# Down rows dealt by the load, block products that add on in PSUM, and one split for two token tiles

## The chip, the cores and the metric

The kernel runs on one core of one Trainium2 chip. A core has a tensor engine (PE, with the weight loads shown apart as PEld), a vector engine (VectorE, DVE in the profile), a scalar engine (ScalarE, ACT), GpSimd (POOL) and SyncE (SP), which here issues nearly all transfers. Transfers run on 16 DMA engines. The time is device microseconds for one execution of the program, and the kernel before takes 1070.54 us (median of three runs, 1070.43 to 1071.01).

## The reference

Two layers work on 256 tokens of 1024 features. Each layer has a feed-forward block, a mixer (gated short convolution, a chunked linear recurrence, multi-scale pooling), cross attention to 256 memory rows, and a second feed-forward block; each of the four ends in a residual and a layer normalization. All inputs and weights are 32-bit floats.

```python
def swiglu(x, w_gate, w_up, w_down):
    return (jax.nn.silu(x @ w_gate) * (x @ w_up)) @ w_down
...
    h = x
    for l in range(DEPTH):
        h = layer_norm(ALPHA * h + 0.5 * swiglu(h, ffn1_gate[l], ffn1_up[l], ffn1_down[l]),
                       ln_g[l, 0], ln_b[l, 0])
        z = h @ w_in[l]
...
        mix = jnp.concatenate([y_conv, y_rec, y_pool], axis=-1) @ w_out[l]
        h = layer_norm(ALPHA * h + mix, ln_g[l, 1], ln_b[l, 1])
        h = layer_norm(ALPHA * h + cross_attn(h, mem, ca_q[l], ca_k[l], ca_v[l], ca_o[l]),
                       ln_g[l, 2], ln_b[l, 2])
        h = layer_norm(ALPHA * h + 0.5 * swiglu(h, ffn2_gate[l], ffn2_up[l], ffn2_down[l]),
                       ln_g[l, 3], ln_b[l, 3])
    return h
```

The inner width of a feed-forward block (FFN) is 2816: gate and up are 1024 x 2816, down is 2816 x 1024. The change touches the four FFNs, and in one place the loading of the memory rows.

## The kernel before

**Split numbers.** Every operand of a large product is kept as a high part in a reduced format (`hi`, written by ScalarE as a cast) and a low part (`lo`, the rest, subtracted by VectorE). `split` (L60 to L62) issues the two. A product of two such operands is three matmuls: high by high, high by low, low by high (`mm_rows`). `product` walks the moving operand so that neighbouring columns of PSUM come from the two halves of the weight columns: column c of the first half and column c of the second half lie beside each other.

**Loads.** `load` fetches a weight block in tiles of 128 partitions x 1024 numbers (512 KB), two to a call's step. They land in a ring of six `raw` buffers; each is split into `whi` and `wlo`, rings of eight. A load is issued by SP in the order of the program, waits there until its `raw` buffer is free, and holds back the loads and the small transfers that stand behind it on SP. For the down weights one tile is 128 neighbouring rows of 4 KB.

**An FFN in chunks.** The width is cut into five chunks of 512 columns and one of 256. For most chunks (`first`, `hidden`) PE makes the gate product (48 matmuls for both token tiles of 128) and the up product (48). `activate` (L436) writes Silu of the gate sums from PSUM to `sg`, and `gated` (L440) multiplies by the up sums. Both do so in two instructions for a token tile, because the order of the columns in PSUM and the order wanted in `sg` don't fit one access pattern. Then `turn` transposes: four small SP transfers (128 KB each) deal `sg` out over the partitions into the tile `dealt`, VectorE transposes 32 x 32 blocks into `square`, and `split` makes the high and low parts `ah`, `al` for the down product. It does this for one token tile after the other.

**Down products.** `both(c, u)` multiplies half a chunk (two tiles of down rows, 24 matmuls) into four sums `dn` that stay in PSUM through the FFN. The half chunks are interleaved with the products of later chunks. The last three (both halves of chunk 4, the first of chunk 5, the 256 wide one) are kept for `tail`, which `finish` calls for each token tile and each half of the columns; one such call reads all six remaining down tiles, then the normalization of that part follows.

**Chunks by seven products.** Chunk 4 (and chunk 2 in three of the four FFNs) is made by `by_seven`: two token tiles against gate and up, seen as a product of 2 x 2 blocks, by seven block products in place of eight. `bx` holds sums and differences of blocks of x; `parts_of` adds weight blocks in place (L597) and splits them. A product (`run`) is 12 matmuls into a PSUM tile. `put` (L619) adds or subtracts a product from PSUM to a 512 wide tile in SBUF. Four products go into four PSUM tiles; three more go into new ones of the same ring of four, and are added to the sums in SBUF by `left`, after which Silu and the multiplication follow in another tile `sg`, and `turn`.

**What sets the order.** A scheduler puts the instructions of each engine into one order before the run; the engines keep that order and wait for each other by semaphores. The order for the matmuls of the mixer and of the kernel's start is written by hand.

## Time and profile before

| | before |
|---|---|
| median of three runs | 1070.54 us |
| profiled execution, span | 1068.8 us |
| PE busy | 1059.3 us (99%), 5966 matmuls |
| DVE busy | 946.3 us (89%) |
| ACT busy | 642.4 us (60%) |
| DMA, mean rate | 217 GB/s |
| DMA queue of SP and its kind, share of 16 engines | 64.8% |

The span runs from the first to the last instruction of the profiled execution; the device time of the runs lies some 2 us above it. Busy time counts an engine's instructions, and for PE neighbouring matmuls overlap. In a row of the groups of instructions the line comes first, then the engine, the operation, what it writes and reads (`whi<-raw`), the shapes and the count; behind the first bar busy time and the mean of one in ns, behind the second the idle time of the engine just before these instructions and what ended it. The chain of waits lists the work that ended last, followed back from the end. In a row of stretches the two last numbers are the share of the 16 DMA engines that was busy and the GB/s moved.

### The profile page before, as it was taken

The page shows a single profiled execution, that of the slowest core. Times are in us where ns is not written, and L with a number is a line of the kernel's source. Part 1 is how long each engine was busy: PE and PEld are TensorE (multiplying, and loading weights), DVE is VectorE, ACT ScalarE, POOL GpSimd, SP SyncE. Part 2 cuts the span into 40 slices and gives each one's busy share as a digit, 9 for nine tenths or more (in the row PEclk, how much of TensorE's full clock was granted, in tenths as well). Part 3 has the DMA queues.
Part 4 walks back from the last instruction along what each step waited for, and adds up shares of the span by engine and source line. Part 5 has one row for each costly group of instructions (what it writes and reads, how often), then busy time and mean ns, then how long its engine had stood idle before and what let it go on. Part 6 is the DMA issues. An engine that isn't in the chain of part 4 may idle for free.

```text
span 1068.8 us, 16312 instructions
## 1 busy us (share of the span) xinstructions
PE 1059.3 (99%) x5966; PEld 937.7 (88%) x5966; DVE 946.3 (89%) x1318; ACT 642.4 (60%) x916; POOL 66.4 (6%) x114
## 2 busy tenths in 40 slices
PE   9999999999999999999999999999999999999997
PEld 7888888889899888888888888888898998888886
DVE  6977997998988799999799999788989787999996
ACT  7555664666557565656575557566764665656660
POOL 9700001000000000000000000010000000000000
PEclk9999999999999999999999999999999999999999
DMA  9997484755574575848675865856536665759461
GB/s 362 262 307 256 129 288 165 249 176 174 170 278 167 178 252 194 290 167 218 238 272 184 256 254 183 290 179 216 196 126 213 241 227 181 257 156 334 134 223 40
DMA packets 130895, 231.90 MB, mean 217 GB/s; under 512 B 9408, under 2 KB 48608, under 8 KB 130816
## 3 DMA queue, kind: packets, MB, share of 16 engines
q1 hardware_dynamic: 129024, 228.49, 64.8%
q0 software_dynamic: 1216, 1.20, 0.5%
q8 instruction: 47, 0.77, 0.3%
q10 hardware_dynamic: 576, 1.18, 0.3%
q14 instruction: 32, 0.26, 0.1%
HBM read 216.15 MB, written 1.05 MB: 203 GB/s over the span
## 4 chain that ended last, share of the span: by engine, by line
PE 99%; DMA 0%; DVE 0%; issue 0%; DVEq 0%
PE acc L105 65%; PE dn L105 31%; PE acc L172 1%; PE dn L923 1%; PE dn L982 0%; DMA h<-in_x_dram 0%; PE acc L491 0%; PE dn L981 0%; PE dn L971 0%; PE acc L1047 0%; PE dn L888 0%; DVE h L358 0%; DVE h L353 0%; PE dn L472 0%; DVE st L338 0%
## 5 line engine op out<-in xcount | busy, mean ns | idle before, releaser
L61 ACT CAST whi<-raw 128x1024 fp32r<-128x1024 f32 (+1 forms) x438 | 442.9, 1042 | 197.5 <-DVE raw L597 54.9
L62 DVE TENSOR_TENSOR wlo<-raw,whi 128x1024 fp32r<-128x1024 f32 (+1 forms) x438 | 515.7, 1209 | 32.6 <-ACT whi L61 29.0
L105 PE MATMUL acc<-whi,xT 128*128 128x512 f32 x1032 | 312.9, 380 | 0.0
L105 PEld LDWEIGHTS acc<-whi,xT 128*128 128x128 f32 x1032 | 195.1, 189 | 27.5
L105 PE MATMUL acc<-wlo,xT 128*128 128x512 f32 x516 | 195.6, 379 | 0.0
L105 PE MATMUL acc<-xT,whi 128*128 128x512 f32 x576 | 142.3, 383 | 0.2
L105 PE MATMUL dn<-whi,ah 128*128 128x512 f32 x346 | 131.5, 380 | 0.0
L105 PE MATMUL dn<-wlo,ah 128*128 128x512 f32 x346 | 131.2, 379 | 0.0
L105 PE MATMUL dn<-whi,al 128*128 128x512 f32 x346 | 131.2, 379 | 0.0
L105 PEld LDWEIGHTS acc<-xT,whi 128*128 128x128 f32 x576 | 104.0, 190 | 12.5 <-ACT whi L61 0.7
L105 PEld LDWEIGHTS acc<-wlo,xT 128*128 128x128 f32 x516 | 97.5, 189 | 13.8
L105 PE MATMUL dn<-whi,xT 128*128 128x512 f32 x288 | 87.9, 381 | 0.0
L105 PEld LDWEIGHTS acc<-xT,wlo 128*128 128x128 f32 x576 | 75.5, 191 | 3.9
L105 PE MATMUL acc<-xT,wlo 128*128 128x256 f32 x576 | 75.9, 275 | 0.0
L105 PEld LDWEIGHTS dn<-whi,al 128*128 128x128 f32 x346 | 65.4, 189 | 9.2
L105 PEld LDWEIGHTS dn<-wlo,ah 128*128 128x128 f32 x346 | 65.4, 189 | 9.2
L105 PEld LDWEIGHTS dn<-whi,ah 128*128 128x128 f32 x346 | 65.4, 189 | 9.1
L350 POOL TENSOR_TENSOR rs<-rs,nhalf 128x1 f32<-128x1 f32 x16 | 14.9, 930 | 833.6 <-DVE rs L346 598.1
L597 DVE TENSOR_TENSOR raw<-raw 128x1024 f32<-128x1024 f32 x56 | 66.2, 1217 | 0.4
L105 PEld LDWEIGHTS dn<-whi,xT 128*128 128x128 f32 x288 | 54.4, 189 | 7.7 <-DVE xT L62 0.3
L105 PE MATMUL dn<-wlo,xT 128*128 128x512 f32 x144 | 54.6, 379 | 0.0
L332 DVE SCALAR_TENSOR_TENSOR h<-h,dn 128x512 f32<-128x512 f32 x31 | 21.2, 683 | 32.9 <-PE dn L105 32.9
(234 smaller groups left out, 1277.5 us busy)
## 6 DMA issues: line engine op xcount, KB each, us to landing
raw<-in_ffn_up_dram SPq DMA_DIRECT2D x88, 512.0 KB, 5.3
raw<-in_ffn_down_dram SPq DMA_DIRECT2D x88, 512.0 KB, 6.6
raw<-in_ffn_gate_dram SPq DMA_DIRECT2D x84, 512.0 KB, 5.1
raw<-in_w_in_dram SPq DMA_DIRECT2D x48, 512.0 KB, 4.7
dealt<-sg SPq DMA_DIRECT2D x80, 128.0 KB, 4.7
raw<-in_ca_k_dram SPq DMA_DIRECT2D x16, 512.0 KB, 4.9
raw<-in_w_out_dram SPq DMA_DIRECT2D x16, 512.0 KB, 4.5
raw<-in_ca_v_dram SPq DMA_DIRECT2D x16, 512.0 KB, 5.3
```

What stands on the lines that cost most here:

```text
L61: nc.scalar.copy(hi, src)
L62: lows.append(nc.vector.tensor_tensor(lo, src, hi.bitcast(F32), op=ALU.subtract))
L105: nc.tensor.matmul(o, w, x, start=start, stop=stop)
L172: nc.tensor.transpose(pt[:, k, :], src[:, (4 * j + k) * P : (4 * j + k + 1) * P], unit)
L332: nc.vector.scalar_tensor_tensor(v, v, ALPHA / scale, sums(y[i][n]), op0=ALU.mult, op1=ALU.add, accum_out=None if junk is None else st[:, ...
L350: nc.gpsimd.tensor_tensor(rs, rs, nhalf[:, 0:1], op=ALU.pow)
L597: nc.vector.tensor_tensor(r[i], r[i], plus[i], op=ALU.add)
L923: nc.tensor.matmul(o[g, hh, :], kc[:, hh, g], x, start=True, stop=True)
```

## The change

Four things change together.

1. *Down rows.* For chunks 0 to 4 a down tile no longer holds 128 neighbouring rows. `load` gets a flag `dealt`: of 256 rows, tile b takes the rows a*64 + b*32 + j, with a from 0 to 3 and j from 0 to 31. With the inner index in this order, `activate` and `gated` write `sg` in one pattern, one instruction for a token tile.
2. *Block products.* Products five to seven start from what stands in PSUM (`more`, no start flag) and add onto products one, three and four there. The order of the three becomes: gate's lower block, up's lower block, the sum of blocks. Two additions to SBUF tiles go away, e and f lie in one tile `ef`, and the last multiplication is done for both tiles in one instruction, in place in `sg`.
3. *Turn.* The transposes of both token tiles write one tile, and one `split` follows.
4. *Tiles.* The pool's two `up` buffers of 512 numbers become one of 1024, which `square`, `halves`, `up` and the memory rows' `turned` share.

```diff
-    def load(src, k0, nk, c0, ncol, fine=False):
+    def load(src, k0, nk, c0, ncol, fine=False, dealt=False):
...
             for b in range(0, step, part):
-                loads.append(nc.sync.dma_start(
-                    raw[b // half][:, b % half : b % half + part, :],
-                    src[(a + b) * P : (a + b + part) * P, c0 : c0 + ncol].rearrange("(k p) c -> p k c", p=P),
-                ))
+                to = raw[b // half][:, b % half : b % half + part, :]
+                if dealt:
+                    rows = src[a * P : (a + step) * P, c0 : c0 + ncol].rearrange("(a k j) c -> k a j c", a=4, j=32)
+                    loads.append(nc.sync.dma_start(to[:, 0, :], rows[b]))
+                else:
+                    loads.append(nc.sync.dma_start(
+                        to, src[(a + b) * P : (a + b + part) * P, c0 : c0 + ncol].rearrange("(k p) c -> p k c", p=P)
+                    ))
...
             def ordered(v):
-                return v.rearrange("p (a k j) -> p k a j", a=4, j=32)
-
-            def by_two(v, o):
-                o = o.rearrange("p (n a j m) -> p m n a j", n=2, a=4, m=2)
-                return [(ordered(v)[:, 2 * m : 2 * m + 2], o[:, m]) for m in range(2)]
+                return v.rearrange("p (a m q) -> p a m q", a=4, m=2)
+
+            def in_order(o):
+                return o.rearrange("p (a q m) -> p a m q", a=4, m=2)
 
             def activate(s, i, og):
-                for v, o in by_two(s[:, i, :], og):
-                    nc.scalar.activation(v, o, AF.Silu)
+                nc.scalar.activation(ordered(s[:, i, :]), in_order(og), AF.Silu)
 
             def gated(s, i, ou):
-                for v, o in by_two(s[:, i, :], ou):
-                    nc.vector.tensor_tensor(v, o, v, op=ALU.mult)
+                v = ordered(s[:, i, :])
+                nc.vector.tensor_tensor(v, in_order(ou), v, op=ALU.mult)
...
+                d = fp.tile([P, NT, 4, P], F32, tag="up", name="square", bufs=1)
                 for i in range(NT):
-                    d = fp.tile([P, 4, P], F32, tag="up", name="square")
                     nc.vector.transpose(
-                        d.rearrange("p k (b r) -> p b k r", b=4), x[:, :, i, :].rearrange("p b (k j) -> p b k j", k=4)
+                        d[:, i].rearrange("p k (b r) -> p b k r", b=4),
+                        x[:, :, i, :].rearrange("p b (k j) -> p b k j", k=4),
                     )
-                    split(ah[:, :, tok(i)], al[:, :, tok(i)], d)
+                d = d.rearrange("p i k t -> p k i t")
+                split(*(y.rearrange("p k (i t) -> p k i t", i=NT) for y in (ah, al)), d)
...
                 s = activations()
+                ef = fp.tile([P, NT, CHUNK], F32, tag="up", name="halves", bufs=1)
+                e, f = ef[:, 0, :], ef[:, 1, :]
                 o = [acc((P, CHUNK)) for _ in range(4)]
                 run(o[0], part_of_x(0, 0), parts_of(w00))
                 run(o[2], bx[0], parts_of(w00, w01))
+                nc.scalar.copy(ordered(s[:, 0, :]), in_order(o[0]))
                 run(o[1], bx[1], parts_of(w00, w11))
-                e = half_sum()
-                put(e, o[1], ALU.add, g[0])
+                put(s[:, 0, :], o[1], ALU.add, s[:, 0, :])
                 run(o[3], bx[2], parts_of(w01, w11))
-                put(g[1], o[3], ALU.add, e)
-                f = half_sum()
-                put(f, o[2], ALU.subtract, g[1])
-                put(e, o[2], ALU.subtract, e)
-                o = [acc((P, CHUNK)) for _ in range(3)]
-                run(o[0], bx[3], parts_of(w11))
-                run(o[1], part_of_x(0, 1), parts_of(w10))
-                run(o[2], part_of_x(1, 1), parts_of(w00, w10))
+                put(s[:, 1, :], o[3], ALU.add, s[:, 0, :])
+                put(f, o[2], ALU.subtract, s[:, 1, :])
+                run(o[0], part_of_x(0, 1), parts_of(w10), True)
+                run(o[2], bx[3], parts_of(w11), True)
+                run(o[3], part_of_x(1, 1), parts_of(w00, w10), True)
 
                 def left():
-                    put(e, o[0], ALU.add, e)
-                    for i in range(NT):
-                        put(g[i], o[1 + i], ALU.add, g[i])
-                    s = fp.tile([P, NT, CHUNK], F32, tag="spare2", name="sg", bufs=1)
-                    for i, u in enumerate((e, f)):
-                        v = ordered(s[:, i, :])
-                        nc.scalar.activation(v, g[i].rearrange("p (k a j) -> p k a j", a=4, j=32), AF.Silu)
-                        nc.vector.tensor_tensor(v, v, u.rearrange("p (k a j) -> p k a j", a=4, j=32), op=ALU.mult)
+                    put(e, o[2], ALU.subtract, s[:, 0, :])
+                    put(s[:, 1, :], o[3], ALU.add, s[:, 0, :])
+                    activate(s, 0, o[0])
+                    nc.scalar.activation(s[:, 1, :], s[:, 1, :], AF.Silu)
+                    nc.vector.tensor_tensor(s, s, ef, op=ALU.mult)
                     return turn(s)
...
             def slab(c, u):
-                w = load(down, c * 4 + 2 * u, 2, 0, DM)
+                w = load(down, c * 4 + 2 * u, 2, 0, DM, dealt=c < len(chunks) - 1)
```

More of the change, by code (lines that the diff above doesn't have):

```diff
@@ L100, in halves, with product @@
         )
-    def product(o, w, x, start, stop):
+    def product(o, w, x, start, stop, more=False):
         x = x.rearrange("p (h c) -> p c h" if len(x.shape) == 2 else "p r (h c) -> p r c h", h=2)
         o = o.rearrange("p (c h) -> p c h" if len(o.shape) == 2 else "p r (c h) -> p r c h", h=2)
-        nc.tensor.matmul(o, w, x, start=start, stop=stop)
+        nc.tensor.matmul(o, w, x, start=start, stop=stop, skip_group_check=more)
     def sums(o):
@@ L126, in add, with mm_rows @@
         nc.vector.tensor_tensor(dst, o[:, 0], dst, op=ALU.add)
-    def mm_rows(o, xh, xl, wh, wl, start, stop):
-        product(o, xh, wh, start, False)
-        product(o, xh, wl, False, False)
-        product(o, xl, wh, False, stop)
+    def mm_rows(o, xh, xl, wh, wl, start, stop, more=False):
+        product(o, xh, wh, start, False, more)
+        product(o, xh, wl, False, False, more)
+        product(o, xl, wh, False, stop, more)
     def tok(i):
@@ L608, in part_of_x, with run @@
                     return xTh[:, d, tok(i)], xTl[:, d, tok(i)]
-                def run(o, x, w):
+                def run(o, x, w, more=False):
                     for k in range(4):
                         wh, wl = w.at(k, slice(0, CHUNK))
-                        mm_rows(o, x[0][:, k, :], x[1][:, k, :], wh, wl, k == 0, k == 3)
-                def half_sum():
-                    return fp.tile([P, 4, P], F32, tag="up", name="half").rearrange("p k t -> p (k t)")
+                        mm_rows(o, x[0][:, k, :], x[1][:, k, :], wh, wl, k == 0 and not more, k == 3, more)
@@ L618, in put @@
                 def put(o, a, op, b):
-                    nc.vector.tensor_tensor(halves(o), sums(a), halves(b), op=op)
+                    nc.vector.tensor_tensor(ordered(o), in_order(a), ordered(b), op=op)
                 s = activations()
-                g = [s[:, i, :] for i in range(NT)]
+                ef = fp.tile([P, NT, CHUNK], F32, tag="up", name="halves", bufs=1)
+                e, f = ef[:, 0, :], ef[:, 1, :]
                 o = [acc((P, CHUNK)) for _ in range(4)]
                 run(o[0], part_of_x(0, 0), parts_of(w00))
-                nc.scalar.copy(halves(g[0]), sums(o[0]))
```

8 lines of the change are left out of this document (4 added, 4 removed).

## The prediction

> **What bounds the kernel now.** I read the page from its head to the chain, then the waits of the tensor engine, then the transfers.
>
> ```profile
> span 1068.8 us, 16312 instructions
> PE 1059.3 (99%) x5966; PEld 937.7 (88%) x5966; DVE 946.3 (89%) x1318; ACT 642.4 (60%) x916; POOL 66.4 (6%) x114
> ...
> PEclk9999999999999999999999999999999999999999
> ...
> DMA packets 130895, 231.90 MB, mean 217 GB/s; under 512 B 9408, under 2 KB 48608, under 8 KB 130816
> ...
> q1 hardware_dynamic: 129024, 228.49, 64.8%
> ...
> PE 99%; DMA 0%; DVE 0%; issue 0%; DVEq 0%
> ```
> ```profile
> 1057.48 4.03 PE acc L105 x36
> ```
> ```profile
> PE dn L472 <- DVE kTh L467: 1.5, 1, 1.5
> PE acc L491 <- DMA h<-in_x_dram: 0.5, 1, 0.5
> ```
>
> The chain is PE for 99% of the span, at a full granted clock, the second fence is its last stretch of PE work (start, length), and the third the whole list of PE's waits: two, at the start. All that is not PE busy is 1068.8 - 1059.3 = 9.5 us, 7.3 of them after that last stretch, at 1061.5, in the final normalization and the output. The profiled execution (1068.8 us of span) lies 1.7 us below the median of 1070.54, so the sum is made as an addition and put on the median. The matmuls are the same in number and shape after the change. So it can win little; it loses where a weight tile comes late. That turns the question to the loads, which take 64.8% of 16 DMA engines as a mean.
>
> **What the edits take off the vector and scalar engines** (groups, kept apart by shape):
>
> ```profile
> L62 DVE TENSOR_TENSOR wlo<-raw,whi 128x1024 fp32r<-128x1024 f32 x430 | 510.4, 1219 | 32.5 <-ACT whi L61 29.0 <-PE acc L105 1.9
> L597 DVE TENSOR_TENSOR raw<-raw 128x1024 f32<-128x1024 f32 x56 | 66.2, 1217 | 0.4
> L62 DVE TENSOR_TENSOR al<-square,ah 128x512 fp32r<-128x512 f32 x40 | 25.7, 682 | 0.4
> L440 DVE TENSOR_TENSOR sg<-acc,sg 128x256 f32<-128x256 f32 x52 | 19.3, 415 | 0.0
> L619 DVE TENSOR_TENSOR half<-acc,sg 128x512 f32<-128x512 f32 x14 | 9.6, 684 | 0.0
> L649 DVE TENSOR_TENSOR sg<-sg,half 128x512 f32<-128x512 f32 x14 | 9.3, 685 | 0.4 <-ACT sg L648 0.4
> ...
> L61 ACT CAST whi<-raw 128x1024 fp32r<-128x1024 f32 x430 | 438.2, 1049 | 197.2 <-DVE raw L597 54.9 <-PE dn L105 53.5 <-PE acc L105 35.5
> L61 ACT CAST ah<-square 128x512 fp32r<-128x512 f32 x40 | 24.3, 621 | 19.0 <-DVE square L453 18.9
> L436 ACT ACTIVATE sg<-acc 128x256 f32<-128x256 f32 x48 | 16.0, 382 | 5.7 <-PE acc L105 5.5
> ```
>
> - One eviction for a token tile: 52 of 0.415 us become 26 of about 0.684 (the 512-wide product from PSUM), -3.8 us on DVE; 52 Silu halves of 0.382 (these 48 and 4 more of another pool) become 26 of at most 0.621, -3.7 us on ACT.
> - Products that add on in PSUM: each of 7 block-product chunks loses 2 of its 7 512-wide additions, 14 x 0.684 = -9.6 us; its two multiplications of 0.685 become one of about 1.217, -1.1 us.
> - One split for both token tiles: 40 x 0.682 to 20 x 1.219, -2.9 us on DVE; 40 x 0.621 to 20 x 1.049, -3.9 us on ACT. Both transposes now precede the split, which delays the first half by under 2 us; its reader comes a projection later (over 10 us).
>
> Together some -17.4 us on DVE and -7.6 on ACT, costed at nothing, since PE is the cover and does not wait for them. If that cover goes, it goes because PE and DVE wait for loads, and then less DVE work does not shorten the wait.
>
> **The accumulation's new waits.** Product six now adds onto the sum that the fourth addition (f) still reads, so after product four two additions must be through before it, with one weight split between them in the changed order: 2 x 0.684 + 1.219 = 2.6 us, and product five covers 12 matmuls of 0.216 = 2.6 us. Before, two products covered three additions. I take 0; the other end is another split in front, 1.2 us x 7 = 8.5 us.
>
> **The moved rows of the down weights.** This is the part that decides. 80 of the 88 down loads keep bytes, row length and their issuer, SP, but read four runs of 32 rows, 64 rows apart: the source's outermost count goes from 128 to 4. No load of the trace has such a pattern; the outermost counts on SP's queue are 128 or, at the dealt tiles, 32. The list of issues (the first two rows and the last of 28, 586 issues in all; the last figure is the median to landing):
>
> ```profile
> raw<-in_ffn_up_dram SPq DMA_DIRECT2D x88, 512.0 KB, 5.3
> raw<-in_ffn_down_dram SPq DMA_DIRECT2D x88, 512.0 KB, 6.6
> ...
> rows<-in_pool_scale_dram POOLq DMA_DIRECT2D x1, 2.0 KB, 4.8
> ```
>
> The page's 9408 packets under 512 B are 16.05 for each issue, which I read as one completion write per engine and transfer: so far every transfer uses all 16. So the price lies between 16 engines (nothing changes) and one engine for each outermost row block, four. Rates per engine come from three stretches:
>
> ```profile
> 1033.50:1039.50 6.00, 6.00 (x38) 5.49 (x37) 5.50 (x8) 4.71 (x7) 0.00 (x0) 1.00 0.66 271
> 970.00:990.00 20.00, 20.00 (x94) 17.54 (x93) 17.43 (x17) 13.13 (x17) 0.00 (x0) 1.00 1.02 368
> 990.00:1010.00 20.00, 20.00 (x95) 17.51 (x94) 19.97 (x24) 11.51 (x13) 0.00 (x0) 1.00 0.25 77
> ```
>
> The last two columns are the share of the 16 engines and GB/s. Down rows of 4 KB: 271/16/0.66 = 25.7 GB/s for an engine; the mix with 2 KB rows: 22.5; mostly dealt tiles: 19.3. A 512 KB load gives 32,768 B to each of 16 engines, 1.28 us (down) or 1.45 (gate, up); on four it gives 131,072 B, 5.1 us, while the others idle. I take four: what all the listed hardware-queue loads share, counts on both sides that 16 divides, is what this one loses.
>
> The Trainium skill has a rule for it (DMA: Bandwidth & Descriptors, the section Why a DMA increments its semaphore by 16 and not by 1): a transfer runs on the largest number of engines up to 16 that divides the outermost counts of both sides. By it 128 and 4 give four engines; the 16 small packets per issue agree with it for the old patterns, and no run here yet shows four.
>
> Now one FFN, with each engine serving its queue in order. Where the first changed load is issued, and where PE needs the last:
>
> ```profile
> 24.99 1.59 SPq L77 DMA_DIRECT2D raw<-in_ffn_down_dram  x2
> ...
> 387.39 2.08 SPq L77 DMA_DIRECT2D raw<-in_ffn_down_dram  x2
> ...
> 554.97 2.08 SPq L77 DMA_DIRECT2D raw<-in_ffn_down_dram  x2
> ...
> 913.69 2.08 SPq L77 DMA_DIRECT2D raw<-in_ffn_down_dram  x2
> ...
> 994.05 2.61 SPq L450 DMA_DIRECT2D dealt<-sg  x4
> ```
> ```profile
> 155.68 18.13 PE dn L105 x84
> ...
> 514.34 18.13 PE dn L105 x84
> ...
> 681.97 18.13 PE dn L105 x84
> ...
> 1040.64 16.84 PE dn L105 x78
> ```
> ```profile
> raw<-in_ca_o_dram SPq DMA_DIRECT2D x16, 512.0 KB, 3.8
> ```
>
> The second fence starts with a half chunk of down products (24 matmuls, 18.13/84 = 0.216 us each, 5.2 us), and then the tail, whose first sum reads all of its six tiles within 18 matmuls: the last at +15 x 0.216 = 3.2 us. So PE needs the last tile at 164.1, 522.8, 690.4 and 1049.1: 139.1, 135.4, 135.4 and 135.4 us after the first changed issue. In that time the four engines must pass 20 changed loads, 20 x 5.1 = 102.2 us; 28 of gate and up, 28 x 1.45 = 40.6; two down and two normalization loads, 5.1; and 20 dealt tiles of 8,192 B per engine, 0.43 each, 8.5: 156.4 us. Add the fixed part of a load (3.8 - 1.28 = 2.5 us), cast and split (1.05 + 1.22): 161.2 us. The last tile is late by 22.1 us once and 25.8 three times, **99.5 us**. The lead of loads over PE is already spent in this: it stands in the window. With 16 engines the same work is 80 us, in a window of 135.
>
> Then the dealt tiles stand in the same queues. The one issued at 994.05 has 13 changed loads, some 21 others and 12 dealt ahead of it since 914.7: 66 + 30 + 5 us, so it lands near 1020, where its transposes ran here:
>
> ```profile
> 1003.02 1.30 DVE L453 STREAM_TRANSPOSE square<-dealt 128x512 f32<-128x512 f32 x2
> ```
> ```profile
> 1008.93 0.33 SPq L77 DMA_DIRECT2D raw<-in_ffn_down_dram  x1
> ```
>
> DVE stands there some 17 us, with the block product's splits queued behind it in order, and with them the release of the raw buffer for the next down load, 5.9 us after the transposes in this trace (1008.93, below). Of those 17 us only what empties the queues counts: they run dry at 1020 plus two normalization loads, 1022.6, and are fed again at 1026 plus 1.0: 4.4 us, four times, **17.6 us**. The price of a cold PE after its waits I bound by the start's row, 7 x (0.651 - 0.380) = 1.9 us, four times **7.6 us**, and zero:
>
> ```profile
> L472 PE MATMUL dn<-kTh 128*128 128x512 f32 x7 | 3.7, 651 | 1.5 <-DVE kTh L467 1.5
> L105 PE MATMUL dn<-whi,ah 128*128 128x512 f32 x346 | 131.5, 380 | 0.0
> ```
>
> Issuing: the new pattern may take SP what a dealt tile takes, 2.61/4 = 0.65 us; 20 in an FFN are 13 us in 135, behind transfers of 5.1 us each, so nothing.
>
> Sum: 99.5 + 17.6 + 7.6 = 125 us, and 1070.5 + 125 = 1195; the 28 gate and up loads at 25.7 GB/s too (0.17 us less each, 19 us in four FFNs) would make it 1176, and I take a value nearer to the sum, **1190 us**.
>
> **Rivals.**
> 1. The split over the engines does not follow the outermost count, and all 16 are used: then nothing on the path changes, 1070 us. For it: bytes and row lengths are the same. Against: nothing in the trace but the missing example. It decides if 8 engines or more are used, since 20 x 2.55 + 54.2 = 105 us fits the window.
> 2. Faster, by DVE's 17.4 us: PE would have to be waiting for DVE. Its list of waits has 2.0 us at the start, and of the 9.5 us without PE most are the first loads and the last normalization; 9.5 - 7.3 = 2.2 us at most, 1068.4, and part of that is the start.
> 3. 16 engines, but the accumulation's wait comes out at its upper end: 1079 us. For it: DVE is 89% busy and in order.
> 4. Four engines that keep only the mean rate of the whole run: 228.49 MB/(16 x 0.648 x 1068.8 us) = 20.6 GB/s. The window's 3.83 MB per engine take 186 us, 30 more per FFN, 1310 us. Against: that mean is of 16 engines crowding one memory.
>
> **How the numbers follow.** Four engines as summed 0.80, rival 1 0.10, rival 2 0.02, rival 3 0.03, rival 4 0.05. The likeliest alone spans 1100 (three quarters of the lateness made up by loads that start earlier than those of this trace, no cold clock) to 1285 (most of the way to rival 4); 1078 to 1285 takes in rival 3 and leaves some 2 in 10 out. Faster by over 0.2% (2.1 us, about what a measurement here can tell) is rival 2's 0.02, the same is rival 1's 0.10, slower is the rest, 0.88.
>
> **What would show it.** Packets under 512 B fall by 80 x 12 = 960 to about 8450; the changed loads' median to landing rises from 6.6 us to well over 10; PE waits for ACT and DVE on down tiles at the four tails, 20 to 30 us each, and its granted clock dips there; DVE waits for dealt tiles. DVE's busy time falls by some 17 us. The prediction is wrong if the small packets stay at 9408, or if the queues turn out to be fed so far ahead that the tails find their tiles.

## The result, and the profile after

The changed kernel takes **1305.13 us** (median of 4 runs, 1302.22 to 1315.31), the kernel before in the same session 1070.76 us (1070.43 to 1071.01). The ratio is 1.220, with a 95% interval of 1.217 to 1.223: 234 us slower. The forecast was 1190 us, 120 us slower, with 1078 to 1285 around it: the direction was right, the size was half of what was measured, and the time lies outside the range.

The page of the changed kernel, the lines that answer to those of before (busy times and their share; the granted clock in 40 slices; packets; the load queue; the chain by engine and by line):

```profile
span 1302.8 us, 16237 instructions
...
PE 1138.3 (87%) x5966; PEld 972.3 (75%) x5966; DVE 937.0 (72%) x1251; ACT 632.8 (49%) x870; POOL 66.2 (5%) x114
...
PEclk9898987999999999979699997969999999999798
...
DMA packets 129935, 231.90 MB, mean 178 GB/s; under 512 B 8448, under 2 KB 47648, under 8 KB 129856
...
q1 hardware_dynamic: 128064, 228.49, 55.9%
...
PE 41%; DMA 30%; DVE 15%; SPq 7%; issue 3%; ACT 3%; DVEq 0%; ACTq 0%
PE acc L110 27%; DMA raw<-in_ffn_down_dram 18%; PE dn L110 12%; DVE wlo L62 7%; SPq L453 7%; DMA dealt<-sg 6%; DMA raw<-in_ffn_gate_dram 5%; DVE raw L602 2%; ACT whi L61 2%; DMA raw<-in_ffn_up_dram 1%; DVE al L62 1%; DVE square L456 1%; DVE sg L443 1%; PE acc L177 1%; DVE sg L621 0%
```

The chain was PE for 99% of the span; now PE holds 41% of it and transfers 30%, the down loads alone 18%. The small packets are 8448, which is 9408 less 80 x 12: each of the 80 changed loads writes 4 completions and not 16. The bytes are the same. PE's busy time rose by 79.0 us for the same 5966 matmuls, while its granted clock dips (line PEclk; its mean is 0.928, against 0.998 before). The waits of the changed kernel (waiter, its line, releaser: total us, times, longest):

```profile
ACT whi L61 <- DMA raw<-in_ffn_down_dram: 221.5, 48, 11.1
DVE wlo L62 <- ACT whi L61: 199.6, 78, 5.7
...
DVE square L456 <- DMA dealt<-sg: 62.5, 14, 11.3
```
```profile
PE dn L110 <- ACT ah L61: 67.2, 12, 12.2
PE acc L110 <- DVE wlo L62: 27.7, 9, 8.1
PE acc L110 <- DVE sg L621: 23.6, 7, 4.3
PE dn L110 <- ACT whi L61: 11.1, 7, 2.2
```

The two waits for transfers in the kernel before:

```profile
ACT whi L61 <- DMA raw<-in_ffn_down_dram: 20.3, 15, 3.7
...
DVE square L453 <- DMA dealt<-sg: 7.8, 4, 3.6
```

ACT waits 222 us for down tiles (20 before), VectorE waits for ACT, VectorE stands 63 us for dealt tiles (8 before), and PE, which waited for nothing after the start, now waits for ACT and VectorE. The third PE row is of another kind: PE waits until VectorE has read a sum onto which a product is to be added. The end of the chain (start, length, what):

```profile
1246.71 3.93 SPq L453
1250.64 0.05 issue
1250.69 2.77 SPq L453
...
1254.16 6.24 SPq L453
...
1260.50 14.21 DMA raw<-in_ffn_down_dram
```

The last changed load is issued at 1260.50 and takes 14.2 us. Ahead of it SP stood in the issues of four dealt tiles. They are the last four of their FFN; in the kernel before, the last four (1025.67, line 450 there) took 2.64 us in all:

```profile
1245.88 14.52 SPq L453 DMA_DIRECT2D dealt<-sg  x4
```
```profile
1025.67 2.64 SPq L450 DMA_DIRECT2D dealt<-sg  x4
```

Of SP's 544 issues, 66 lasted longer than 1.5 us, 222.6 us in all; before, 3 did, 4.7 us.

So the candidates for the 234 us were: the four engines' work; SP's standing in line; the way the dealt tiles wait; the accumulation; and PE's slower clock. The experiments take the first and the fourth apart from the rest. No run changes the clock alone.

### The profile page after: what moved, and what is told of

Its sections match the earlier page's. It is cut to its first block, busy times and chain, and to the rows that moved or that the text cites. A ratio compares the mean times of both kernels' runs of the same rounds, so it can differ in the third digit from the quotient of the medians.

```text
span 1302.8 us, 16237 instructions
## 1 busy us (share of the span) xinstructions
PE 1138.3 (87%) x5966; PEld 972.3 (75%) x5966; DVE 937.0 (72%) x1251; ACT 632.8 (49%) x870; POOL 66.2 (5%) x114
## 2 busy tenths in 40 slices
DMA packets 129935, 231.90 MB, mean 178 GB/s; under 512 B 8448, under 2 KB 47648, under 8 KB 129856
## 3 DMA queue, kind: packets, MB, share of 16 engines
q0 software_dynamic: 1216, 1.20, 0.5%
## 4 chain that ended last, share of the span: by engine, by line
PE 41%; DMA 30%; DVE 15%; SPq 7%; issue 3%; ACT 3%; DVEq 0%; ACTq 0%
PE acc L110 27%; DMA raw<-in_ffn_down_dram 18%; PE dn L110 12%; DVE wlo L62 7%; SPq L453 7%; DMA dealt<-sg 6%; DMA raw<-in_ffn_gate_dram 5%; DVE raw L602 2%; ACT whi L61 2%; DMA raw<-in_ffn_up_dram 1%; DVE al L62 1%; DVE square L456 1%; DVE sg L443 1%; PE acc L177 1%; DVE sg L621 0%
## 5 line engine op out<-in xcount | busy, mean ns | idle before, releaser
L110 PE MATMUL acc<-whi,xT 128*128 128x512 f32 x1032 | 320.6, 385 | 30.1 <-DVE sg L621 23.6
L110 PEld LDWEIGHTS acc<-whi,xT 128*128 128x128 f32 x1032 | 197.6, 191 | 62.5 <-issue 31.9
L110 PE MATMUL dn<-whi,ah 128*128 128x512 f32 x346 | 147.8, 427 | 78.3 <-ACT ah L61 67.2
L110 PE MATMUL dn<-whi,al 128*128 128x512 f32 x346 | 146.3, 423 | 6.1 <-DVE al L62 6.1
L110 PE MATMUL dn<-wlo,ah 128*128 128x512 f32 x346 | 146.5, 423 | 4.7 <-DVE wlo L62 4.7
L110 PEld LDWEIGHTS dn<-whi,ah 128*128 128x128 f32 x346 | 73.9, 214 | 98.3 <-ACT ah L61 73.0
L110 PEld LDWEIGHTS dn<-whi,al 128*128 128x128 f32 x346 | 73.1, 211 | 24.2 <-DVE al L62 12.9
L110 PEld LDWEIGHTS dn<-wlo,ah 128*128 128x128 f32 x346 | 73.6, 213 | 19.8 <-DVE wlo L62 8.2
L110 PE MATMUL acc<-wlo,kTh 128*128 128x512 f32 x112 | 50.6, 452 | 27.2 <-DVE wlo L62 27.1
L456 DVE STREAM_TRANSPOSE square<-dealt 128x512 f32<-128x512 f32 x40 | 26.0, 689 | 62.5 <-DMA dealt<-sg 62.5
L355 POOL TENSOR_TENSOR rs<-rs,nhalf 128x1 f32<-128x1 f32 x16 | 14.9, 930 | 1058.2 <-DVE rs L351 770.7
```

The costliest lines, as they stand in the source:

```text
L110: nc.tensor.matmul(o, w, x, start=start, stop=stop, skip_group_check=more)
L355: nc.gpsimd.tensor_tensor(rs, rs, nhalf[:, 0:1], op=ALU.pow)
L456: nc.vector.transpose(d[:, i].rearrange("p k (b r) -> p b k r", b=4), x[:, :, i, :].rearrange("p b (k j) -> p b k j", k=4),)
```

## The experiments

### The other parts of the change: plain rows

```diff
-                w = load(down, c * 4 + 2 * u, 2, 0, DM, dealt=c < len(chunks) - 1)
+                w = load(down, c * 4 + 2 * u, 2, 0, DM, dealt=False)
```

The order of instructions on every engine is that of the changed kernel.

> The changed kernel with the down rows fetched in plain order (the pairing of rows and activations is left out, so the output differs); all other parts of the change stand. Theory: the other parts cost and bring next to nothing, 1068 to 1071 us. Rival (the accumulation's wait or the shared buffers cost): 1079 us or more. Rival (they bring DVE's 17 us): 1054 to 1066 us.

Measured 1082.2 us, ratio 1.0108 (1.0093 to 1.0123): the second reading. The rest of the change costs 11.6 us. PE's waits, the whole list of this run, and its busy line:

```profile
PE acc L110 <- DVE halves L621: 5.3, 7, 0.8
PE acc L110 <- DVE sg L621: 2.6, 7, 0.4
PE dn L477 <- DVE kTh L472: 1.5, 1, 1.5
PE acc L496 <- DMA h<-in_x_dram: 0.5, 1, 0.5
```
```profile
PE 1063.0 (98%) x5966; PEld 937.2 (87%) x5966; DVE 935.5 (87%) x1251; ACT 639.2 (59%) x870; POOL 66.4 (6%) x114
```

The last two rows were there before. The first two are new, 7 times each, once for each block-product chunk: the two accumulating products whose sums VectorE still reads. They stop PE for 7.9 us, and PE is busy 3.7 us longer (1063.0 against 1059.3): 11.6 us, the whole difference of the two spans (1080.4 less 1068.8).

### The accumulation alone

The edit to the kernel with plain rows (lines that only write to another tile are left out):

```diff
...
-                run(o[0], part_of_x(0, 1), parts_of(w10), True)
-                run(o[2], bx[3], parts_of(w11), True)
-                run(o[3], part_of_x(1, 1), parts_of(w00, w10), True)
...
+                o = [acc((P, CHUNK)) for _ in range(3)]
+                run(o[0], part_of_x(0, 1), parts_of(w10))
+                run(o[1], bx[3], parts_of(w11))
+                run(o[2], part_of_x(1, 1), parts_of(w00, w10))
...
+                    put(e, o[1], ALU.add, e)
+                    for i in range(NT):
+                        put(s[:, i, :], o[2 * i], ALU.add, s[:, i, :])
...
```

> The changed kernel with plain rows (pairing left out), and the three late products in PSUM sums of their own again, added on VectorE as before the change; one pattern, one split and the shared buffers stay. Theory (the 11.6 us that plain rows leave are PE's wait until VectorE has read a sum onto which a product is to be added): 1069 to 1071 us. Rival (they come from the shared buffers or the one split for both token tiles): 1080 to 1083 us.

Measured 1071.25 us, ratio 1.0003 (0.9994 to 1.0011). The loss of plain rows went with the accumulation. The scheduler's order changes with the edit too, but the list of waits above names the same cause, and here PE's waits are again the two of the start. The one eviction pattern, the one split and the shared buffers together cost and bring nothing that can be measured.

### The loads alone, in the kernel before

The load function of the changed kernel in the kernel before; nothing else:

```diff
-                w = load(down, c * 4 + 2 * u, 2, 0, DM)
+                w = load(down, c * 4 + 2 * u, 2, 0, DM, dealt=c < len(chunks) - 1)
```

> The kernel before, with one edit: the down loads of all chunks but the last fetch four runs of 32 rows (rows and activations paired wrongly). Theory: the loads alone carry the whole loss, 1300 to 1310 us. Rival (half of the loss is from the other parts, the forecast of 1190 was right for the loads): about 1190 us.

Measured 1292.7 us, ratio 1.207 (1.206 to 1.209), 222 us over before, with every engine's instructions in the order of the kernel before. This is 7 us under the range that was expected, which gave the loads the whole loss. With plain rows the rest of the change costs 11.6 us, and the four-run loads add 222.9 to that (1305.1 less 1082.2). The two parts add up.

### How many engines: 2, 8 and 16

```diff
-                    rows = src[...].rearrange("(a k j) c -> k a j c", a=4, j=32)
+                    rows = src[...].rearrange("(a k j) c -> k a j c", a=8, j=16)
```

with a=16, j=8 and a=2, j=64 in the two other runs. The orders of instructions on all engines are those of the changed kernel.

> The changed kernel, where a changed load fetches eight runs of 16 rows instead of four runs of 32 (so rows and activations are paired wrongly; sizes, bytes, instructions and their order are those of the changed kernel). Theory (the outermost count of the source sets how many engines serve a load, and their work is what delays): 8 engines, 65,536 B each, 2.55 us at 25.7 GB/s; 20 x 2.55 + 54.2 = 105 us of engine work per FFN in a window of 135: about 1070 us, at most 1075. Rival (a source in runs is slow in itself, or slow to issue, whatever the number of engines): no better than the changed kernel, about 1300 us. Rival (the extra over the forecast is SP's waiting at each load that is not yet taken): some tens of us above 1070, 1090 to 1150.

> The changed kernel, where a changed load fetches sixteen runs of 8 rows (rows and activations paired wrongly; all else as in the changed kernel). Theory (number of engines): 16 engines as before, 1066 to 1070 us, and the packets under 512 B are 9408 again. Rival (runs are slow in themselves): near 1300 us.

> The changed kernel where a changed load fetches two runs of 64 rows (rows paired wrongly): two engines, 262,144 B each, 10.2 us a load at 25.7 GB/s. Theory (engine time): in the changed kernel's fourth FFN the load queue was busy 168 us of 173; each of 20 loads is 5.1 us longer, 102 us an FFN, 408 us in all: 1700 to 1730 us. Rival (the loss grows with the loads' own share of packets, slower at fewer engines): above 1800.

The packets of the three runs, of 8, 16 and 2 runs in a load:

```profile
DMA packets 130256, 231.90 MB, mean 203 GB/s; under 512 B 8769, under 2 KB 47969, under 8 KB 130177
```
```profile
DMA packets 130896, 231.90 MB, mean 213 GB/s; under 512 B 9409, under 2 KB 48609, under 8 KB 130817
```
```profile
DMA packets 129775, 231.90 MB, mean 140 GB/s; under 512 B 8288, under 2 KB 47488, under 8 KB 129696
```

The small packets are 9408 less 80 x 8, 0 and 14, to within one: a source with an outermost count of 8, 16 or 2 runs on 8, 16 or 2 engines. This is the rule of the Trainium skill (DMA: Bandwidth & Descriptors, Why a DMA increments its semaphore by 16 and not by 1), and four runs here agree with it. The times are 1143.7, 1091.4 and 1661.1 us. All three miss what the theory gave (at most 1075; at most 1070; 1700 to 1730). Eight engines should have fitted the window and lost 61.5 us over plain rows. That time lies in the range of the third reading, SP's waiting, but SP's issues over 1.5 us are 12 there, 34.6 us in all, and the run down_on_pool below speaks against it too. That the number of engines orders the loss is shown; the sum that turns it into time was wrong. What the trace's packet records say of it comes below.

The run of 16 engines lost 9.2 us over plain rows, although all engines work. Its 4 KB packets, those of the changed loads and all others together, have a median of 232 ns, against 159 in the changed kernel and with plain rows. Its 16 runs of rows start 64 KB apart.

### Sixteen engines, and the right rows

Two ways to the right rows with 16 engines, each with the accumulation and with sums of their own (the edit shown above). The first issues each changed load as four, one for each run of 32 rows:

```diff
-                    loads.append(nc.sync.dma_start(to[:, 0, :], rows[b]))
+                    for q in range(4):
+                        loads.append(nc.sync.dma_start(to[q * 32 : q * 32 + 32, 0, :], rows[b][q]))
```

> The changed kernel, where each changed load is issued as four loads of 32 rows, one for each run: the same rows on the same partitions. The outermost count of each is 32, so 16 engines serve each. Theory (number of engines and slower packets of a source in strides): the loss falls to what the kernel with plain rows has left, 1082 us, or to 1091 if the slower packets of the 16-engine run were from rows that lie apart; range 1078 to 1095. Rival (loads in runs cost by themselves, or 240 more issues on SP hold up what stands behind): 1110 us or more.

> Both mends together, a kernel that computes all that is asked: four loads of 32 rows for each changed load, and the three late products in sums of their own. Theory: the two losses are separate and both go, 1068 to 1072 us, the time of the kernel before. Rival: 240 more issues on SP, or the slower packets, leave 5 to 15 us: 1075 to 1085.

Measured 1224.0 (1.141, 1.139 to 1.144) and 1213.8 us (1.134, 1.132 to 1.136): both missed. The small packets were 13248, 16 for each load, so all engines did work. But four times the issues make the scheduler, which orders by its own costs, write another order on PE, ACT and VectorE. The same four loads with plain rows, in the same order on every engine, tell whether the rows or the order count:

```diff
-                    rows = src[...].rearrange("(a k j) c -> k a j c", a=4, j=32)
+                    rows = src[...].rearrange("(k a j) c -> k a j c", a=4, j=32)
```

> Four loads of 32 rows for each down tile as in the kernel of four loads, in the same order of instructions on every engine, but of 128 rows that lie together (pairing left out). Theory (the scheduler's order with four times the issues carries the 142 us that the kernel of four loads lost over plain rows): 1215 to 1225 us again. Rival (rows that lie apart do): about 1082 us.

Measured 1224.1 us. The rows that lie apart have no part in it. Its waits show where the time goes:

```profile
ACT ah L61 <- DVE square L456: 116.0, 14, 15.2
...
PE acc L110 <- ACT whi L61: 28.9, 27, 2.2
PE dn L110 <- ACT whi L61: 27.1, 9, 4.4
```

ACT stands 116 us in front of the cast of a transposed tile (22 us with plain rows and one load), and PE waits for the weight casts queued behind it. How much of this is the order, how much the 240 more issues on SP, and how much the slower packets of such loads (4 KB in 219 and 223 ns in the median of the two kernels) was not tried apart. The load queue is not short of room there: by the count shown further down, it has a packet in flight for 109 us of an FFN's stretch of 170, and nothing for 61.

The second way moves the rows otherwise. Partition p takes rows 2p and 2p + 1 of a slab's 256, so a load's source has an outermost count of 128, and one pattern still evicts a token tile:

```diff
-                    rows = src[...].rearrange("(a k j) c -> k a j c", a=4, j=32)
+                    rows = src[...].rearrange("(p k) c -> k p c", p=P)
...
-                return v.rearrange("p (a m q) -> p a m q", a=4, m=2)
+                return v.rearrange("p (a t j) -> p a t j", a=4, j=32)
...
-                return o.rearrange("p (a q m) -> p a m q", a=4, m=2)
+                return o.rearrange("p (a j t) -> p a t j", a=4, j=32)
...
+                if c < len(chunks) - 1:
+                    return w, *(y.rearrange("p (k m) t -> p m k t", m=2)[:, u] for y in (ah, al))
```

> The changed kernel with another order of the rows that one pattern evicts as well: partition p takes rows 2p and 2p+1 of a slab's 256, so a changed load's source has an outermost count of 128 (every second row), and the activations are written in the order that fits. It computes all that is asked, and it issues each load once, in the changed kernel's order. Theory (number of engines; the kernel of four loads was slow because the scheduler put ACT's and PE's work in another order): the 223 us go, 1080 to 1092 us, the upper end if rows that lie apart are slow as in the 16-engine run. Rival (a kernel in which the rows are really reordered is slow whatever the number of engines, as the four loads suggest): 1150 us or more.

> The same with the three late products in PSUM sums of their own. Theory: both losses gone, 1068 to 1075 us, at best the time before or 2 us under it. Rival: the slower packets of rows that lie apart leave some 9 us, 1076 to 1082.

Measured 1081.96 us (1.0106, 1.0092 to 1.0119) and, with sums of their own, 1071.08 us (1.0002, 0.9993 to 1.0011). Both as the theory had it. The page of the first:

```profile
DMA packets 130896, 231.90 MB, mean 215 GB/s; under 512 B 9409, under 2 KB 48609, under 8 KB 130817
...
q1 hardware_dynamic: 129024, 228.49, 64.9%
```

So the down rows may be reordered, and one pattern may evict a tile, at no cost in this order, whose outermost count is 128. That 16 divides the count is not enough for that: the run with a count of 16 lost 9.2 us. The order brings nothing either: the kernel stands where it stood before, as PE is the bound.

### SP's line: the dealt tiles, then the loads, on GpSimd's queue

```diff
-                    nc.sync.dma_start(x[a * 32 : a * 32 + 32], s[:, :, a * P : (a + 1) * P])
+                    nc.gpsimd.dma_start(x[a * 32 : a * 32 + 32], s[:, :, a * P : (a + 1) * P])
```

> The changed kernel with one edit: the transfers of the dealt tiles are issued on GpSimd's queue instead of SP's, so they wait neither behind SP's standing issues nor behind the loads in SP's queue. Theory (the four engines' work per FFN sets the end: 20 loads of 32 packets of 207 ns each, 6.6 us a load): little changes, 1270 to 1310 us. Rival (SP standing in its issues, 223 us of it, holds up the dealt tiles and with them VectorE, and that is what doubles the loss): 1180 to 1230 us, about the forecast.

Measured 1305.4 us (1.218, 1.214 to 1.222), no change, although VectorE's wait for dealt tiles falls from 62.5 to 28.2 us. But with this edit the scheduler also writes another order on PE, VectorE and ACT, and the four loads showed that an order can cost time. So the run shows that the edit as a whole brings nothing; that the dealt tiles' place in SP's line is free is not shown. Then the changed loads themselves on GpSimd's queue:

```diff
-                    loads.append(nc.sync.dma_start(to[:, 0, :], rows[b]))
+                    loads.append(nc.gpsimd.dma_start(to[:, 0, :], rows[b]))
```

> The changed kernel with the changed loads issued on GpSimd's queue, so that SP never stands in one and the other loads and the dealt tiles are issued past them. Theory (four engines' work sets the end; every other load needs these four engines too): 1270 to 1320 us. Rival (SP's order and its standing issues double the loss): 1180 to 1230 us. If GpSimd's queue spreads a load over engines in another way, the packets under 512 B differ from 8448 and the time falls below both.

Measured 1271.7 us (four runs, 1257.6 to 1280.1; 1.190, 1.184 to 1.196), at the low end of the first reading, two runs below it. SP's issues over 1.5 us fell from 66 to 2, from 222.6 us to 7.5, and of the 234 us about 201 stayed. So most of the loss does not hang on SP's standing. PE's order is that of the changed kernel, VectorE's and ACT's are not, and it isn't a clean undoing in another way: on GpSimd's queue the loads carry many more small packets,

```profile
DMA packets 161616, 232.04 MB, mean 185 GB/s; under 512 B 40128, under 2 KB 79328, under 8 KB 161536
```

40128 in place of 8448, so the 25 to 48 us that it won can't be put down to SP.

### A window as a whole, or each load by itself

Eight engines should have fitted. Two runs ask what a four-run load costs where the FFN's window has room; a third gives the kernel with eight engines sums of their own for the late products, by the edit shown above. The edits of the first two:

```diff
-                w = load(down, c * 4 + 2 * u, 2, 0, DM, dealt=c < len(chunks) - 1)
+                w = load(down, c * 4 + 2 * u, 2, 0, DM, dealt=c < 2)
```
```diff
-                if dealt:
+                if dealt and b == 0:
```

> The changed kernel with the four-run loads in the first two of an FFN's five chunks alone, 8 loads in place of 20 (the other chunks take plain rows, so their pairing is left out). Theory (an FFN's engine work against its window: 8 x 6.7 + 12 x 1.45 + 59 = 130 us in 135): hardly any loss beyond the 11.6 us of the accumulation, 1080 to 1095 us. Rival (each four-run load is late by itself, whatever the window): 0.4 of 223 us, about 1170 us.

> The changed kernel, where only the first tile of each pair of down tiles comes by a four-run load and the second by a plain one (its rows are paired wrongly): 10 changed loads in an FFN instead of 20, spread evenly. Theory A (a stretch of four-run loads is late when its work exceeds what PE uses up meanwhile, about 27 us a chunk: 4 x 5.1 + 8 us and more do, 2 x 5.1 do not): nearly all goes, 1082 to 1110 us. Theory B (each four-run load costs its own 2.8 us): 0.5 x 223 = 112 us remain, about 1194 us, with two_chunks (8 loads, 101 us) as the measure.

> The run with eight engines (1144 us, rows paired wrongly), with the three late products in sums of their own. PE's waits on VectorE's reading of the sums were 31 us there and 8 us with plain rows. Theory (with eight engines the engines' work, 20 loads of about 3.6 us and 59 us of the rest, 131 us, just fits the window of 135, and what is left of the loss is VectorE late behind dealt tiles, and PE behind VectorE at the accumulation): about 1080 to 1100 us. Rival (the loss of eight engines comes from the loads themselves): only the 11.6 us go, 1132 us.

Measured 1182.8, 1184.1 and 1164.7 us. With 8 and with 10 four-run loads in an FFN in place of 20, 101 and 102 us are lost over plain rows: 3.1 and 2.5 us for each load, against 2.8 with all 20. Both times the reading by each load comes near and the window is wrong; that a spread of the loads would help was wrong too. The third run fell outside both readings: with sums of their own the eight-engine kernel became slower, by 21 us. Its order of instructions is another one, the same as with plain rows and sums of their own (1071.25 us), and why that order suits late loads worse stays open.

The packet records answer the rest. I counted, from the first to 8 us past the last issue of the 20 down loads of an FFN that the change touches, how long at least one packet of the load queue was in flight, and how long none was (us, mean of the four FFNs; the loss is the run's time less 1082.2, a quarter of it):

```
kernel                      stretch  in flight  none   loss per FFN
before                       124.5     102.4    22.0
plain rows                   125.6     101.3    24.3      0
rows by two                  125.6     103.0    22.6     -0.1
16 engines (runs of 8)       127.7     109.9    17.8      2.3
8 engines (runs of 16)       141.7     127.8    13.9     15.4
two chunks on four engines   149.7     134.8    14.9     25.1
first of two, four engines   151.2     144.6     6.6     25.5
changed kernel, 4 engines    177.7     172.4     5.3     55.7
2 engines (runs of 64)       263.0     258.1     4.9    144.7
```

Three things are to be read. A changed load adds in-flight time nearly as its engines' bytes say: (127.8 - 101.3)/20 = 1.3 us at eight engines, 3.6 at four, 7.8 at two, where the forecast's rate gives 1.28, 3.8 and 8.9. With 8 or 10 such loads on four engines it is more, 4.2 and 4.3. The time with nothing in flight, which such loads could fill, was 22 to 24 us of an FFN's stretch, not 55. And only part of it was used: the stretch grows by the added in-flight time less the idle time that goes, 26.5 - 10.4 = 16.1 us at eight engines (15.4 lost) and 71.1 - 19.0 = 52.1 at four (55.7 lost, the rest after the last issue). This sum holds by the way it is counted; what the runs add is that the loss of each row is nearly the growth of its stretch. It is less so in two runs that are not in the table: with the four-run loads in the kernel before the stretch is 168.6 us and grows by 44.1 of the 55.5 us lost in an FFN, and with the dealt tiles on GpSimd's queue it is 166.8 us and grows by 41.2 of 55.8.

The page's own windows say the same more roughly. Before the change, from the first changed issue of the last FFN to its tail, and in the changed kernel from that issue to the landing of its last down tile (the last two columns: share of the 16 engines, GB/s):

```profile
913.70:1040.60 126.90, 126.90 (x605) 111.57 (x604) 121.42 (x134) 77.95 (x94) 0.00 (x0) 1.00 0.69 228
```
```profile
1095.30:1274.70 179.40, 147.94 (x634) 122.81 (x633) 118.63 (x118) 73.78 (x81) 0.00 (x0) 0.91 0.53 161
```

0.69 of 126.9 us was busy before: 87.6 us of each engine's time.

### PE's own account

PE gives a second account of the same time. The changed kernel and the one with plain rows have the same order on every engine, so each matmul can be set beside itself. Of the 222.4 us between their spans PE stands for 147.1 (164.5 us not busy against 17.4) and is busy for 75.3 us longer (1138.3 against 1063.0). All of it comes in the four FFNs, 64.5, 54.2, 54.8 and 48.8 us, and between them nothing is given back.

87.5 of the 147.1 us of standing fall ahead of the end of the stretches counted above, inside the chunks, and 59.6 at the tails behind it. With eight engines 32.8 of 37.7 us fall inside the chunks, and with two chunks on four engines all of it. After its waits the granted clock is half for 3.4 to 23.9 us at a time, 188 us in the changed kernel in all; before, only in the last 6.8 us of the trace. From PE's longest wait at each tail on, the slower matmuls alone take 24.3 us in the four tails together. The other 51 us fall into stretches where the chain of waits runs mostly over transfers, VectorE and SP (PE's products into `acc` are 14 and 10% of it in the last two FFNs), so how much of them adds to the time is not shown.

## Why the prediction had the direction right and half the size

**Right.** The number of engines was the part that decides. Four engines stand in the 8448 small packets. Every second row, which keeps 16 engines, loses nothing over plain rows, and the four-run loads put into the kernel before lose 222 us. That each load takes 5.1 us was near: it adds 3.6 us in flight where 3.8 were forecast. Also right: the one pattern, the one split and VectorE's saving move nothing; the packet count, the waits for dealt tiles and the dips of the clock came as listed. The time to landing of the changed loads can't be read: the trace of the changed kernel has none for them.

**The step that failed** is the lateness, 99.5 us, in the sentence "With 16 engines the same work is 80 us, in a window of 135". Its work of 80 us was bytes at the best rates that the trace shows. The same trace has its load queue in flight for 102 us of an FFN's stretch of 124.5 (in the forecast's own window of the last FFN, 100.5 of 135.4). The forecast's added work (156.4 less 80, 76 us) was close to the 71 measured; its cover of 55 us was 24, and of these 5 stayed unused. 71.1 - 19.0 = 52.1 us four times are 208 of the loss.

The forecast also let the loads use this cover over a whole FFN, so that only the last tile is late, at the tail. PE's waits show otherwise: 87.5 of 147.1 us of standing come inside the chunks, before the tail, and with eight engines or two chunks nearly all of it does, although 13.9 and 14.9 us of an FFN's stretch still have nothing in flight. That loads can't run ahead far enough, with six raw buffers and engines that work in order, would explain it, but no run changes the number of buffers: this is argued, not shown.

One count was off the other way. The list of issues has 28 gate and up loads between the changed loads in the first FFN alone, and 25 in each of the other three, so three of the four windows were charged 4.4 us too much by the forecast's own rate.

**The cold PE, 7.6 us,** was sized too small. PE is busy 75.3 us longer than with plain rows, and at the tails alone, where the term was meant, the slower matmuls take 24.3 us. The forecast priced seven matmuls after one wait in an FFN; the runs show many waits, and half a clock for 3.4 to 23.9 us after them. By PE's account the forecast's 117.1 us of lateness and dry queues stand against 147.1 us of standing, and its 7.6 us against up to 75.3. How much of these 75.3 us would be lost without the slower clock, because the loads are late anyway, stays open.

**The dealt tiles, 17.6 us.** As a term of its own it falls. Four times 4.4 us of dry queues were forecast, and the queue is dry for 5.3 us per FFN, but that is what is left of 24. VectorE's waits for dealt tiles are real (62.5 us), and the edit that gave these transfers another issuer, and with it another order on the engines, changed nothing in the time. That they are a part of the same backlog is likely, not shown.

**The accumulation, 0.** This term failed too, and its upper end, 8.5 us, was too low: 11.6 measured, 7.9 of them in PE's list of waits. The forecast counted two additions and one split, 2.6 us, against a product of 2.6 us, and took the tie for no wait. In a kernel whose chain is 99% PE nothing covers what goes over a tie, and the third rival, which priced it at 1079, describes the kernel with plain rows (1082).

**Issuing, nothing.** The single issue is as short as forecast (median 0.61 us). What was not foreseen is that SP stands in it when the loads ahead are not taken. That cost showed as SP's 7% of the chain; the two runs that take transfers off SP gained nothing and 25 to 48 us, neither of them cleanly, so the forecast's zero is nearer than the 223 us of standing suggest.

**Rival 1's threshold**, eight engines or more fit the window, was wrong by the same step: eight engines lose 61.5 us. **Rival 4** (1310 us) came out next to the measured time, in part by luck. Its 186 us of work in an FFN are as far above the 172 us in flight as the forecast's 156 are below. Its rate would add 4.8 us for a changed load, where 3.6 were measured (4.2 and 4.3 in the two runs with fewer such loads). That engines were slower than the forecast's rate is not refuted: a 4 KB packet takes 159 ns in the median in both kernels, but 199 ns in the mean in the changed kernel and 186 before.

**VectorE's saving, 17.4 us.** 10.8 us with plain rows (946.3 to 935.5). Counts by mean durations overstate it, as neighbours overlap: 52 evictions by 0.415 are 21.6 us, and the row's busy time was 19.3.

## What to carry to other kernels

Before a load's rows are reordered, look at the outermost count of both sides of the transfer: a count of 2, 4 or 8 left as many engines at work here, 16 and 128 kept all 16, and the bytes and row lengths that the page of the profile shows do not tell. There was an order here that keeps 128 (every second row), at no cost. And the room that a queue has left is read from the time in which it has nothing in flight, in the trace of before; bytes divided by the best rate promised room that was not there. Where PE is the bound, a delay is not given back later, and the slower clock that follows PE's waits belongs into the sum.

## What the runs showed of the hardware that was not expected

- SP stands in the issue of a transfer while its queue is backed up. Issues over 1.5 us were none with plain rows, 12 with eight engines, 66 with four (up to 6.3 us) and 154 with two, 762.6 us in all, the longest 16.7 us. A transfer that uses all 16 engines stands as well when it is behind such loads, as the dealt tiles do (14.5 us for four, 2.6 before).
- 4 KB packets, those of all loads of a run together, take 159 ns in the median where the changed loads of 128 rows are read from adjacent rows, from every second row, or in runs by two, four or eight engines; 232 ns with 16 runs that start 64 KB apart; 219 and 223 with loads of 32 rows, whether these lie apart or together. The Trainium skill (DMA: Bandwidth & Descriptors, Latency and other measured facts) lists lower rates for copies between tensors in HBM whose row pitches are large powers of two, from 512 KiB up; the rows inside a run of this case lie 4 KB apart, so no run here shows it. The cause of the three slow cases stays open.
- The changed loads, issued from GpSimd's queue, still move 4 KB packets, 128 for a load of 128 rows, but with them come 400 packets of 4 bytes, where SP's queue has 4: 42240 packets for the 80 loads (43456 on its queue, 1216 before).
